# Reordering the four products of a k-tile in an FFN up-projection: wide, narrow, wide, narrow against wide, wide, narrow, narrow

## The chip, the cores and the metric

The kernel runs on one core of one Trainium2 chip, as one program launched once. The metric is the device time of one execution in microseconds. A core has five engines that run their own instruction streams side by side: TensorE (matrix products; in the profile PE, and PEld for the loading of its weights), VectorE (DVE), ScalarE (ACT), GpSimd (POOL), and SyncE (SP), which here issues the transfers from device memory. They wait for one another through semaphores.

## The reference

One layer of a hybrid decoder on 256 tokens of width 2048, in float32. Cut to its steps:

```
h  = rms_norm(x, attn_norm);  z = h @ w_in              # 2048 -> 4384
mix = [causal pooling of z, RWKV-7 time mixing of z]
x  = x + mix @ w_out                                    # 2048 -> 2048
h2 = rms_norm(x, mlp_norm)
x  = x + square(relu(h2 @ w_ffn_up)) @ w_ffn_down       # 2048 -> 8192 -> 2048
gate = sigmoid(rms_norm(x, ple_norm) @ w_ple_gate)
x  = x + gate * (p @ w_ple_proj)
out = rms_norm(x, final_norm)
```

The change touches only `h2 @ w_ffn_up`.

## The kernel before

**Precision.** Every large product is made of three. A float32 operand is split into a high half (rounded to the fast format that TensorE takes, `F32R` in the code) and a low half (the rest), and high x high, high x low and low x high are summed in PSUM, TensorE's accumulator memory, which is divided into banks of 512 float32 columns.

**Staging of weights.** `load_raw` has SyncE bring a panel of 128 x 1024 weights (512 KB) into one of three buffers. `split_w` makes the two halves: ScalarE copies the panel into `wh` in two instructions (line 149), VectorE subtracts to get `wl` in one (line 150). `wh` and `wl` have three buffers each, and the splitting runs at a raised priority, so it goes ahead as far as free buffers allow.

**FFN-up.** `gemm_wide` computes it, transposed: the weights are the stationary operand (128 x 128 at a time) and the normalised activations, already transposed by `transposed("h2")`, are the moving one. A call handles 512 of the 8192 columns, in two halves of 256. For a half, `kq` runs over four panels. A panel holds four k-tiles (a k-tile is 128 of the 2048 rows that are summed over), of 256 columns each. For a k-tile there are two column tiles `ct` of 128 columns, each with two products:

- a wide one (line 997): weights `wh`, moving operand `hl = acts(k)`, the high and low halves of the activations side by side, 256 + 256 columns in two stretches of memory. It writes a whole bank, `bank[:, ct, :]`: high x high in the first 256 columns, high x low in the other 256.
- a narrow one (line 1001): weights `wl`, moving operand the high half alone, 256 columns. It adds to the first 256 columns of the same bank.

The two column tiles have a bank each, and such a pair of banks (`wide_bank`) exists twice, so that one half can be emptied while the next is computed. Each product has a weight load of its own ahead of it; the profile shows these as LDWEIGHTS on PEld.

When a half is done, `consume` (the function `square` in `ffn_half`, lines 1193 and on) lets ScalarE copy the second columns out of the bank, VectorE add the first and apply the squared ReLU, and splits the result for the down-projection.

**Order of the work.** `ffn_half` runs twice. Each time eight calls of `gemm_wide` come first (256 k-tiles, 1024 products), then two calls of `down_sweep`, the down-projection, whose products are all 512 wide (lines 1111 to 1113). These two stretches of `gemm_wide` are called the first and the second FFN half here. Nothing but the loops sets the order around the change. The framework schedules the instructions of each engine by priority and readiness: at the very start of the first FFN half some of the transposes that make `h2` (line 1018) stand between products of lines 997 and 1001.

Other stages used for comparison: `prod_toks` (lines 171 to 173), 512-wide products in the output projection and the gate; `prod_cols` (lines 162 to 164), 256-wide products in the input projection and the pooling; `kept_product` (lines 1266 to 1268), the last gate products, first a run of 512-wide ones, then 256-wide ones.

Of the kernel before, what the change touches and what calls it, by code (L numbers as in the profile page):

```python
# [16 lines left out]
T = 256  # L17
# [23 lines left out]
def trunk(  # L41
# [96 lines left out]
    def load_raw(src, n, name):  # L138
        raw = wp.tile([128, 1024], F32, tag="raw", name=f"raw_{name}")
        nc.sync.dma_start(raw[:, 0:n], src)  # L140
        return raw

    def split_w(raw, name):

        wh = wp.tile([128, 1024], F32R, tag="wh", name=f"wh_{name}")
        wl = wp.tile([128, 1024], F32R, tag="wl", name=f"wl_{name}")
        with tc.high_priority(20000):
            for a in range(2):
                nc.scalar.activation(wh[:, a * 512 : (a + 1) * 512], raw[:, a * 512 : (a + 1) * 512], AF.Copy)  # L149
            nc.vector.tensor_tensor(wl, raw, wh.bitcast(F32), op=ALU.subtract)  # L150
        return [(t_h, t_l) for t_h, t_l in zip((wh[:, 0:512], wh[:, 512:1024]), (wl[:, 0:512], wl[:, 512:1024]))]
# [185 lines left out]
    for kg, (tg, n) in enumerate((("tE", 1), ("tF", 2), ("zk", 3), ("zr", 3), ("zv", 3), ("BK", 2), ("BKt", 2))):  # L337
# [13 lines left out]
        if kg == 4:  # L351
            for tt in range(2):
                for i, q in enumerate((2, 3)):
                    nc.tensor.matmul(
                        sbank[:, tt : tt + 1], sums[q][:, 0, tt * 128 : (tt + 1) * 128], ones[:, 0:1],
                        start=i == 0 and tt == 0, stop=i == 1, skip_group_check=True,
# [623 lines left out]
    def wide_bank(name):  # L980
        return psw.tile([128, 2, 512], F32, tag="wide", name=name)

    def gemm_wide(src, acts, name, consume):

        for half in range(2):
            bank = wide_bank(f"{name}_w{half}")
            for kq in range(4):
                raw = load_raw(src[half, kq].rearrange("p a n -> p (a n)"), 1024, f"{name}{half}_{kq}")  # L990
                for a, (wh, wl) in enumerate(split_w(raw, f"{name}{half}_{kq}")):
                    for b in range(2):
                        k = kq * 4 + 2 * a + b
                        hl = acts(k)
                        for ct in range(2):
                            c = slice(b * 256 + ct * 128, b * 256 + ct * 128 + 128)
                            nc.tensor.matmul(  # L997
                                bank[:, ct, :].rearrange("p (s t) -> p s t", s=2), wh[:, c], hl,
                                start=k == 0, stop=False, skip_group_check=True,
                            )  # L1000
                            nc.tensor.matmul(  # L1001
                                bank[:, ct, 0:T], wl[:, c], hl[:, 0, :], start=False, stop=k == 15, skip_group_check=True
                            )
            consume(half, bank)

# [177 lines left out]
    def ffn_half(hf):  # L1183
        sboxes = {}
        ys = []
        for i in range(8):
            f = hf * 8 + i
            y = fp.tile([128, 2048], F32R, tag="y", bufs=8, name=f"y{f}")

            def square(bi, bank):  # L1190
                r = fp.tile([128, 512], F32, tag="r", bufs=2, name=f"r{f}_{bi}")
                r2 = r.rearrange("p (c t) -> p c t", c=2)
                nc.scalar.activation(r2, bank[:, :, T : 2 * T], AF.Copy)
                nc.vector.tensor_tensor(r2, bank[:, :, 0:T], r2, op=ALU.add)
                nc.vector.scalar_tensor_tensor(r, r, 0.0, r, op0=ALU.max, op1=ALU.mult)
                split_sb(y[:, bi * 512 : bi * 512 + 512], y[:, 1024 + bi * 512 : 1024 + bi * 512 + 512], r)
                if 2 * i + bi in SEVEN:
                    activation_sums(sboxes, 2 * i + bi, r)

            gemm_wide(w_up[f], h2, f"u{f}", square)  # L1200
            ys.append(y)
            if f == 1:
                inv_ms()
# [162 lines left out]
```

## Time and profile before

| what | value |
|---|---|
| time, median of 3 runs | 1199.78 us (1199.17 to 1201.17) |
| the profiled execution: its own time | 1201.35 us |
| the profiled execution: its span | 1199.6 us |
| granted TensorE clock | 0.997 of full speed |
| first product of the first FFN half, first down-projection product behind it | 388.7 us, 567.1 us |
| first product of the second FFN half, first down-projection product behind it | 734.7 us, 915.6 us |

How to read the profile. A row of the groups gives the line, the engine, the operation, what it writes and reads, the shapes and the count; after the bar the busy time in microseconds, the mean duration in nanoseconds, and the idle time of the engine just before these instructions with what ended it. A row of the timeline gives the start in microseconds from the span's start, the duration in microseconds, the engine, the line and the operands. On TensorE the recorded spans of neighbouring products overlap and their ends are modelled, so the pace is read from the distance between starts. The chain that ended last is followed back from the last instruction, and shares are of the span.

### The profile page before, as it was taken

To read this page: it belongs to the slowest core of one execution; us is meant where nothing else is said; L and a number is where in the kernel's file an instruction comes from. 1 tells how busy PE (TensorE), PEld (TensorE's weight loads), DVE (VectorE), ACT (ScalarE), POOL (GpSimd) and SP (SyncE) were. 2 spreads that over 40 slices of the span, in tenths; PEclk is the share of its full clock that TensorE was granted. 3 is DMA by queue.
4 is the path that set the end of the run, shared out by engine and by line. 5 is a ranking of instruction groups with operands and counts; after the bars stand their busy time and mean duration, and the time that the engine had idled before them with its cause. 6 is when DMAs were issued, how large, how long until landed. Compare 5 with 4: busy or idle time off the path is not lost.

```text
span 1199.6 us, 18428 instructions
## 1 busy us (share of the span) xinstructions
PE 1179.5 (98%) x7060; PEld 1010.6 (84%) x7060; DVE 868.5 (72%) x1149; ACT 689.8 (58%) x1276; POOL 18.1 (2%) x69
## 2 busy tenths in 40 slices
PE   8999999999999999999999999999999999999997
PEld 6999988987887888888888788888888888777886
DVE  7687987965656666666878888666667879787552
ACT  6857566566545565555655564454555555668544
POOL 4000010000000000000000000000000000000000
PEclk9999999999999999999999999999999999999999
DMA  6463542354445555555665656655555556766531
GB/s 246 154 201 109 175 144 104 113 198 141 140 163 179 184 185 190 192 191 189 201 201 200 193 195 211 191 181 188 189 184 189 207 194 197 287 231 211 195 120 70
DMA packets 60328, 216.88 MB, mean 181 GB/s; under 512 B 6736, under 2 KB 7120, under 8 KB 59856
## 3 DMA queue, kind: packets, MB, share of 16 engines
q1 hardware_dynamic: 59952, 215.19, 53.4%
q8 instruction: 55, 0.90, 0.3%
q10 hardware_dynamic: 288, 0.52, 0.1%
q14 instruction: 33, 0.27, 0.1%
HBM read 213.59 MB, written 2.10 MB: 180 GB/s over the span
## 4 chain that ended last, share of the span: by engine, by line
PE 81%; DVE 8%; DMA 4%; ACT 4%; issue 2%; SPq 0%; ACTq 0%; DVEq 0%
PE u_w L997 20%; PE u_w L1001 10%; PE d_b L1112 5%; PE d_b L1113 5%; PE d_b L1111 5%; DMA raw_d<-in_w_ffn_down_dram 3%; PE gt_b L171 2%; PE gt_b L173 2%; PE gt_b L172 2%; PE wag_b L331 1%; PE zp_b L171 1%; PE o_b L171 1%; PE o_b L172 1%; PE o_b L173 1%; PE d_w L1112 1%
## 5 line engine op out<-in xcount | busy, mean ns | idle before, releaser
L997 PE MATMUL u_w<-h,wh_u 128*128 128x512 f32 x1024 | 358.8, 395 | 0.0
L1001 PE MATMUL u_w<-h,wl_u 128*128 128x256 f32 x1024 | 287.3, 281 | 0.0
L149 ACT ACTIVATE wh_u<-raw_u 128x512 fp32r<-128x512 f32 x256 | 147.6, 624 | 166.2 <-PE u_w L997 93.1
L150 DVE TENSOR_TENSOR wl_u<-raw_u,wh_u 128x1024 fp32r<-128x1024 f32 x128 | 156.7, 1225 | 115.1 <-ACT wh_u L149 115.1
L997 PEld LDWEIGHTS u_w<-h,wh_u 128*128 128x128 f32 x1024 | 192.0, 187 | 44.8
L1001 PEld LDWEIGHTS u_w<-h,wl_u 128*128 128x128 f32 x1024 | 193.6, 189 | 0.0
L150 DVE TENSOR_TENSOR wl_gt<-raw_gt,wh_gt 128x1024 fp32r<-128x1024 f32 x24 | 29.4, 1225 | 23.9 <-ACT wh_gt L149 23.9
L149 ACT ACTIVATE wh_gt<-raw_gt 128x512 fp32r<-128x512 f32 x48 | 27.8, 631 | 23.0 <-PE gt_b L173 18.8
L1151 DVE TENSOR_TENSOR td<-raw_d 128x512 f32<-128x512 f32 x22 | 15.2, 693 | 31.0 <-DMA raw_d<-in_w_ffn_down_dram 31.0
L162 PE MATMUL zv_b<-hTh,wh_zv 128*128 128x256 f32 x128 | 37.6, 294 | 0.0
L171 PE MATMUL gt_b<-wh_gt,h 128*128 128x512 f32 x96 | 37.5, 390 | 0.0
L162 PE MATMUL zr_b<-hTh,wh_zr 128*128 128x256 f32 x128 | 37.4, 292 | 0.0
L173 PE MATMUL gt_b<-wh_gt,h 128*128 128x512 f32 x96 | 37.4, 389 | 0.0
L172 PE MATMUL gt_b<-wl_gt,h 128*128 128x512 f32 x96 | 37.4, 389 | 0.0
L164 PE MATMUL zr_b<-hTh,wl_zr 128*128 128x256 f32 x128 | 37.0, 289 | 0.1
L163 PE MATMUL zr_b<-hTl,wh_zr 128*128 128x256 f32 x128 | 37.0, 289 | 0.0
L162 PE MATMUL zk_b<-hTh,wh_zk 128*128 128x256 f32 x128 | 36.9, 288 | 0.0
L163 PE MATMUL zk_b<-hTl,wh_zk 128*128 128x256 f32 x128 | 36.3, 284 | 0.5 <-DVE hTl L155 0.5
L164 PE MATMUL zk_b<-hTh,wl_zk 128*128 128x256 f32 x128 | 36.3, 284 | 0.1
L163 PE MATMUL zv_b<-hTl,wh_zv 128*128 128x256 f32 x128 | 36.2, 283 | 0.0
L164 PE MATMUL zv_b<-hTh,wl_zv 128*128 128x256 f32 x128 | 36.2, 283 | 0.0
L154 ACT ACTIVATE wad<-raw_d 128x512 fp32r<-128x512 f32 x22 | 13.9, 632 | 33.7 <-DMA raw_d<-in_w_ffn_down_dram 29.1
(807 smaller groups left out, 3077.6 us busy)
## 6 DMA issues: line engine op xcount, KB each, us to landing
raw_u<-in_w_ffn_up_dram SPq DMA_DIRECT2D x128, 512.0 KB, 3.6
raw_d<-in_w_ffn_down_dram SPq DMA_DIRECT2D x128, 512.0 KB, 4.0
raw_gt<-in_w_ple_gate_dram SPq DMA_DIRECT2D x24, 512.0 KB, 3.5
raw_zk<-in_w_in_dram SPq DMA_DIRECT2D x16, 512.0 KB, 3.3
raw_zr<-in_w_in_dram SPq DMA_DIRECT2D x16, 512.0 KB, 3.4
raw_zv<-in_w_in_dram SPq DMA_DIRECT2D x16, 512.0 KB, 3.2
raw_zp<-in_w_in_dram SPq DMA_DIRECT2D x16, 512.0 KB, 3.3
raw_o<-in_w_out_dram SPq DMA_DIRECT2D x16, 512.0 KB, 3.5
```

The source lines that it names most:

```text
L149: nc.scalar.activation(wh[:, a * 512 : (a + 1) * 512], raw[:, a * 512 : (a + 1) * 512], AF.Copy)
L150: nc.vector.tensor_tensor(wl, raw, wh.bitcast(F32), op=ALU.subtract)
L162: nc.tensor.matmul(o, w_h, ah, start=first and ct % 2 == 0, stop=False, skip_group_check=True)
L163: nc.tensor.matmul(o, w_h, al, start=False, stop=False, skip_group_check=True)
L164: nc.tensor.matmul(o, w_l, ah, start=False, stop=last, skip_group_check=True)
L171: nc.tensor.matmul(o, a_h, wh[:, 0:n], start=first, stop=False)
L172: nc.tensor.matmul(o, a_h, wl[:, 0:n], start=False, stop=False)
L173: nc.tensor.matmul(o, a_l, wh[:, 0:n], start=False, stop=last)
L997: nc.tensor.matmul(bank[:, ct, :].rearrange("p (s t) -> p s t", s=2), wh[:, c], hl, start=k == 0, stop=False, skip_group_check=True,)
L1001: nc.tensor.matmul(bank[:, ct, 0:T], wl[:, c], hl[:, 0, :], start=False, stop=k == 15, skip_group_check=True)
L1111: nc.tensor.matmul(banks[n], ah, wh, start=first, stop=False)
L1112: nc.tensor.matmul(banks[n], ah, wl, start=False, stop=False)
```

## The change

For each k-tile the loop over the two column tiles is split in two: first both wide products, then both narrow ones. Before, the four products of a k-tile go wide (ct 0), narrow (ct 0), wide (ct 1), narrow (ct 1); after, wide (ct 0), wide (ct 1), narrow (ct 0), narrow (ct 1). Into each bank the wide product still goes ahead of the narrow one. Operands, widths, flags and counts are the same.

```diff
                     for b in range(2):
                         k = kq * 4 + 2 * a + b
                         hl = acts(k)
+                        cs = [slice(b * 256 + ct * 128, b * 256 + ct * 128 + 128) for ct in range(2)]
                         for ct in range(2):
-                            c = slice(b * 256 + ct * 128, b * 256 + ct * 128 + 128)
                             nc.tensor.matmul(
-                                bank[:, ct, :].rearrange("p (s t) -> p s t", s=2), wh[:, c], hl,
+                                bank[:, ct, :].rearrange("p (s t) -> p s t", s=2), wh[:, cs[ct]], hl,
                                 start=k == 0, stop=False, skip_group_check=True,
                             )
+                        for ct in range(2):
                             nc.tensor.matmul(
-                                bank[:, ct, 0:T], wl[:, c], hl[:, 0, :], start=False, stop=k == 15, skip_group_check=True
+                                bank[:, ct, 0:T], wl[:, cs[ct]], hl[:, 0, :], start=False, stop=k == 15, skip_group_check=True
                             )
             consume(half, bank)
```

## The prediction

> **What bounds the kernel now.** I began with the page: engine shares, clock, chain, costliest groups.
>
> ```profile
> PE 1179.5 (98%) x7060; PEld 1010.6 (84%) x7060; DVE 868.5 (72%) x1149; ACT 689.8 (58%) x1276; POOL 18.1 (2%) x69
> PEclk9999999999999999999999999999999999999999
> PE 81%; DVE 8%; DMA 4%; ACT 4%; issue 2%; SPq 0%; ACTq 0%; DVEq 0%
> PE u_w L997 20%; PE u_w L1001 10%; PE d_b L1112 5%; PE d_b L1113 5%; PE d_b L1111 5%; DMA raw_d<-in_w_ffn_down_dram 3%; PE gt_b L171 2%; PE gt_b L173 2%; PE gt_b L172 2%; PE wag_b L331 1%; PE zp_b L171 1%; PE o_b L171 1%; PE o_b L172 1%; PE o_b L173 1%; PE d_w L1112 1%
> L997 PE MATMUL u_w<-h,wh_u 128*128 128x512 f32 x1024 | 358.8, 395 | 0.0
> L1001 PE MATMUL u_w<-h,wl_u 128*128 128x256 f32 x1024 | 287.3, 281 | 0.0
> L149 ACT ACTIVATE wh_u<-raw_u 128x512 fp32r<-128x512 f32 x256 | 147.6, 624 | 166.2 <-PE u_w L997 93.1
> L150 DVE TENSOR_TENSOR wl_u<-raw_u,wh_u 128x1024 fp32r<-128x1024 f32 x128 | 156.7, 1225 | 115.1 <-ACT wh_u L149 115.1
> ```
>
> TensorE is busy 98% of the span at full clock, and lines 997 and 1001, the two that the change reorders, hold 30% of the chain that ended last. Neither line ever waits (the last column, 0.0). The engines that feed them do wait: ScalarE sits idle 166.2 us before its 256 weight splits, 93.1 us of it for line 997 to give a buffer back. So in FFN-up only the pace of TensorE's own stream counts, and any nanosecond gained or lost there is a nanosecond of the kernel.
>
> Busy time cannot give that pace, because the recorded spans overlap: 358.8 + 287.3 us is far more than the stage lasts. The pace is the distance between starts. I looked at it in the timeline, three pairs in the first FFN half (near 500 us) and three in the second (near 800 us), and then at the groups by shape over most of either half.
>
> ```profile
> 499.88 0.39 PE L997 MATMUL u_w<-h,wh_u 128*128 128x512 f32 x1
> ...
> 500.92 0.39 PE L997 MATMUL u_w<-h,wh_u 128*128 128x512 f32 x1
> ```
>
> ```profile
> 800.04 0.40 PE L997 MATMUL u_w<-h,wh_u 128*128 128x512 f32 x1
> 800.28 0.28 PE L1001 MATMUL u_w<-h,wl_u 128*128 128x256 f32 x1
> 800.40 0.40 PE L997 MATMUL u_w<-h,wh_u 128*128 128x512 f32 x1
> 800.64 0.28 PE L1001 MATMUL u_w<-h,wl_u 128*128 128x256 f32 x1
> 800.75 0.40 PE L997 MATMUL u_w<-h,wh_u 128*128 128x512 f32 x1
> 800.99 0.28 PE L1001 MATMUL u_w<-h,wl_u 128*128 128x256 f32 x1
> 801.10 0.40 PE L997 MATMUL u_w<-h,wh_u 128*128 128x512 f32 x1
> ```
>
> ```profile
> L997 PE MATMUL u_w<-h,wh_u 128*128 128x512 f32 x491 | 170.3, 391 | 0.0
> L1001 PE MATMUL u_w<-h,wl_u 128*128 128x256 f32 x492 | 137.8, 280 | 0.0
> ```
>
> ```profile
> L997 PE MATMUL u_w<-h,wh_u 128*128 128x512 f32 x505 | 178.5, 399 | 0.0
> L1001 PE MATMUL u_w<-h,wl_u 128*128 128x256 f32 x504 | 141.6, 281 | 0.0
> ```
>
> The first fence is 1.04 us for three pairs: 346.7 ns a pair, 693.3 ns a k-tile (two pairs). The second is 1.06 us: 353.3 ns a pair, 706.7 ns a k-tile; there the distances walk round a cycle of three pairs (0.24, 0.12, 0.24, 0.11, 0.24, 0.11 us). The two group tables (395 to 565 us, then 736 to 914 us) say that this holds all along: the wide product's mean is 391 ns in the one and 399 ns in the other, by the same instructions. So the same code runs at two paces, a settled one and an unsettled one. That is the reading on which everything below rests.
>
> **The change part by part.** The number of products, their widths, weight loads, bytes and DMAs stay. Per k-tile the order wide, narrow, wide, narrow becomes wide, wide, narrow, narrow, on 512 k-tiles (256 in each half). The average pace before is (693.3 + 706.7) / 2 = 700.0 ns, so with c the new distance per k-tile the change is worth 512 x (c - 700.0 ns): every 2 ns of c is 1.0 us.
>
> Neither wide after wide nor narrow after narrow stands in FFN-up before. The nearest rows are elsewhere: long runs of one width, here the last gate products (1174 to 1178 us wide, 1180 to 1186 us narrow), and the places where a run of one width follows the other.
>
> ```profile
> L1267 PE MATMUL gt3a<-gk,h 128*128 128x512 f32 x7 | 2.7, 389 | 0.0
> ```
>
> ```profile
> L1267 PE MATMUL gt3b<-gk,h 128*128 128x256 f32 x14 | 4.0, 283 | 0.0
> ```
>
> ```profile
> 327.95 0.28 PE L164 MATMUL pm<-d,pws 128*128 128x256 f32 x1
> 328.07 0.40 PE L171 MATMUL o2a_b<-wh_o2a,mp 128*128 128x512 f32 x1
> 328.30 0.40 PE L172 MATMUL o2a_b<-wl_o2a,mp 128*128 128x512 f32 x1
> 328.54 0.39 PE L173 MATMUL o2a_b<-wh_o2a,mp 128*128 128x512 f32 x1
> ```
>
> ```profile
> 1178.05 0.39 PE L1268 MATMUL gt3a<-gk,h 128*128 128x512 f32 x1
> ...
> 1178.73 0.39 PE L1268 MATMUL gt3a<-gk,h 128*128 128x512 f32 x1
> 1178.96 0.28 PE L1266 MATMUL gt3b<-gk,h 128*128 128x256 f32 x1
> 1179.07 0.28 PE L1267 MATMUL gt3b<-gk,h 128*128 128x256 f32 x1
> 1179.19 0.28 PE L1268 MATMUL gt3b<-gk,h 128*128 128x256 f32 x1
> ...
> 1179.55 0.28 PE L1268 MATMUL gt3b<-gk,h 128*128 128x256 f32 x1
> ```
>
> A settled wide run goes at (1178.73 - 1178.05) / 3 = 227 ns, a settled narrow run at (1179.55 - 1179.19) / 3 = 120 ns. Two of each make 693.3 ns: exactly the settled pace of the alternating order. So the settled price of a product does not depend on its neighbour, and the order alone cannot go below 693.3 ns. This is the low end: c = 693.3, worth 512 x (-6.7) = -3.4 us. It also says that the wide product's moving operand, which line 997 reads in two separate stretches of 256, costs nothing there.
>
> Out of a settled run the first products of the other width are different. After narrow ones the first two wide take 328.54 - 328.07 = 0.47 us, some 16 ns more than settled; after wide ones the first two narrow take 1179.19 - 1178.96 = 0.23 us, some 10 ns less. The new order is a change of width every two products, so its k-tile by these rows is 0.47 + 0.23 = 0.70 us. The starts are rounded to 10 ns, and the recorded durations give the next digit, since a duration is the distance to the next start plus about 162.5 ns (389 and 227, 283 and 120):
>
> ```profile
> L172 PE MATMUL o2a_b<-wl_o2a,mp 128*128 128x512 f32 x1 | 0.4, 398 | 0.0
> L171 PE MATMUL o2a_b<-wh_o2a,mp 128*128 128x512 f32 x1 | 0.4, 396 | 0.0
> ```
>
> ```profile
> L1267 PE MATMUL gt3b<-gk,h 128*128 128x256 f32 x14 | 4.0, 283 | 0.0
> L1266 PE MATMUL gt3b<-gk,h 128*128 128x256 f32 x1 | 0.3, 278 | 0.0
> ```
>
> 396 + 398 + 278 + 283 - 4 x 162.5 = 705 ns by the durations, 700 ns by the starts; I take 702 ns. The high end for c: the longest distances of the unsettled cycle (800.04 to 800.28 and 800.28 to 800.40 us) for every product, 2 x 240 + 2 x 120 = 720 ns, worth +10.2 us; 706.7 ns, the unsettled pace as it stands, is the nearer of the high values. I choose 702 because only these rows have the new order's own neighbours.
>
> Sum: first half 256 x (702 - 693.3) = +2.2 us, second half 256 x (702 - 706.7) = -1.2 us, together +1.0 us.
>
> The weight loads. One load goes with each product, before and after. Its row starts with the product ahead of it and not sooner:
>
> ```profile
> 500.11 0.28 PE L1001 MATMUL u_w<-h,wl_u 128*128 128x256 f32 x1
> 500.11 0.19 PEld L997 LDWEIGHTS u_w<-h,wh_u 128*128 128x128 f32 x1
> ```
>
> So each wide product covers one load and each narrow one covers one, in either order; the new order changes which load lies under which product, not how many lie under a narrow one. Cost nothing; if the loads did not fit under the narrow ones, the narrow runs at 120 ns would show it, and they have a load each.
>
> The Trainium skill (TensorE: Matmul & The Clock Gate, Part 2, step 1 LDWEIGHTS) has TensorE pull weight loads ahead of running products through a window of 64. By that rule loads would gather under the two wide products and narrow ones would go at their bare pace; the trace does not agree, since the load above starts at 500.11 us with the product just ahead of it.
>
> Waits at the edges of a panel. The low weight half is first needed after two wide products instead of one, 0.23 us later; the high half is released one narrow product (0.12 us) sooner. Neither product has a wait to shorten (0.0 above), so this is worth nothing. The cover is ScalarE's idle time of 166.2 us ahead of its splits; if it were gone, each of the 128 panels would come up to 0.12 us sooner by the earlier release, 15 us in all, a gain that the 0.0 excludes. The PSUM bank's evacuation may start 0.12 us sooner; with two banks and 16 k-tiles (11 us) a half, nobody waits for it. No DMA is moved. Cost nothing.
>
> The profiled execution took 1201.35 us for a span of 1199.6 us; by the sum it becomes 1202.4 us. It lies 1.6 us above the median of the runs, 1199.78 us, so the median becomes 1200.8 us.
>
> **The rivals.** What a measurement of this kernel can tell from no change is 0.2%, 2.4 us, which by 512 x (c - 700) is c below 695.3 or above 704.7 ns.
>
> *The new order settles* in both halves, c = 693.3: 1199.8 - 3.4 = 1196.4 us. For it: every long run of one width settles, and runs of two are nearer to that than alternation. Against it: alternation settles only in the first half, and a fresh change of width every two products is what unsettles the rows above.
>
> *The unsettled cycle takes both halves*, the case on the other side: two wide in a row at the unsettled mean, 399 - 162.5 = 236.5 ns, and narrow ones at the 117 to 120 ns that they have everywhere, c about 706.7 to 713. The place is the first half, which loses its settled pace: 256 x 13.3 = +3.4 us, 1203.2 us, and 1206.4 us at 713. It decides from c = 704.7. For it: the second half does this now, for all its 1024 products. Against it: the transition rows at 700 to 705.
>
> *Loads run ahead* under two wide products, so that narrow ones go at the 113 ns that one has after a wide one (278 - 162.5 = 115.5, 0.11 us by starts): c = 2 x 227 + 2 x 113 = 680, -10.2 us, 1189.6 us. Against it: the load row, and the narrow run returning to 120 ns at once. This is the time that the Trainium skill's window (the page and step above) would allow.
>
> *The order isn't carried out*: the framework schedules TensorE's instructions and may move them. Then 1199.8 us. Against it: the pairs stand in the trace as written.
>
> **How the numbers follow.** Forecast (c about 702, 698 to 707): 0.41, most of it within 0.2%, 0.06 of it slower. Settled in both halves: 0.25. Unsettled in both halves or worse: 0.28. Loads run ahead: 0.03. Not carried out: 0.03. Faster by over 0.2%: 0.25 + 0.03 = 0.28. Within: 0.35 + 0.03 = 0.38. Slower: 0.06 + 0.28 = 0.34. The likeliest is 1200.8 us, with 1198.8 to 1203.4 us as its own range (c 698 to 707). The range of 8 in 10 goes from just under the settled case, 1196.0 us, to 1205.5 us (c about 711), which leaves out the run-ahead case and the dear end of the unsettled one.
>
> **What would show it.** In the groups, lines 997 and the narrow line keep 1024 products each and no idle time. In the timeline a k-tile of four starts spans about 0.70 us, with wide distances of 0.23 to 0.24 us and narrow ones of 0.11 and 0.12 us. Right: both halves at the same pace, the first slower than before and the second faster. Wrong: a wide mean of 389 to 391 ns in both halves (settled), or 399 ns and more in both; a load that starts two products ahead; or idle time that appears before the narrow line.

## The result, and the profile after

| | before | after |
|---|---|---|
| median of 22 runs each | 1200.68 us | 1198.38 us |
| ratio after / before, 95% interval | | 0.9978 (0.9968 to 0.9988) |
| the profiled execution, its span | 1201.35 us, 1199.6 us | 1198.69 us, 1197.0 us |
| first FFN half, first start to first down-projection start | 388.74 to 567.13: 178.4 us | 388.75 to 567.95: 179.2 us |
| second FFN half, likewise | 734.69 to 915.58: 180.9 us | 735.07 to 913.40: 178.3 us |

The kernel became 0.22% faster (0.12 to 0.32%, so 1.4 to 3.8 us of 1200). The forecast was 1200.8 us, 1.0 us more than before and too little to be told from no change.

The page after, the lines that answer to those shown of before (engine shares, chain by line, groups):

```profile
PE 1177.8 (98%) x7060; PEld 1008.1 (84%) x7060; DVE 868.4 (73%) x1149; ACT 689.2 (58%) x1276; POOL 18.6 (2%) x69
PE u_w L997 20%; PE u_w L1002 10%; PE d_b L1113 5%; PE d_b L1112 4%; PE d_b L1114 4%; DMA raw_d<-in_w_ffn_down_dram 4%; PE gt_b L171 2%; PE gt_b L173 2%; PE gt_b L172 2%; PE wag_b L331 1%; PE zp_b L171 1%; PE o_b L171 1%; PE o_b L172 1%; PE o_b L173 1%; PE zp_b L173 1%
L997 PE MATMUL u_w<-h,wh_u 128*128 128x512 f32 x1024 | 321.6, 395 | 0.0
L149 ACT ACTIVATE wh_u<-raw_u 128x512 fp32r<-128x512 f32 x256 | 147.6, 624 | 164.4 <-PE u_w L997 93.9
L1002 PE MATMUL u_w<-h,wl_u 128*128 128x256 f32 x1024 | 201.5, 278 | 0.0
```

The narrow product is now line 1002. The busy times fell from 358.8 to 321.6 us and from 287.3 to 201.5 us, and this says nothing: busy time is the union of spans within a group, and products of one line now overlap each other. The other rows are those of before: 1024 products each, no idle time, ScalarE waiting 164.4 us (166.2).

The pace is in the starts. The timeline of after near 800 us; it merges the two products of a kind into one row:

```profile
799.85 0.63 PE L997 MATMUL u_w<-h,wh_u 128*128 128x512 f32 x2
800.32 0.39 PE L1002 MATMUL u_w<-h,wl_u 128*128 128x256 f32 x2
800.54 0.63 PE L997 MATMUL u_w<-h,wh_u 128*128 128x512 f32 x2
801.01 0.40 PE L1002 MATMUL u_w<-h,wl_u 128*128 128x256 f32 x2
801.24 0.63 PE L997 MATMUL u_w<-h,wh_u 128*128 128x512 f32 x2
```

Two wide ones take 0.47 us, two narrow ones 0.22 and 0.23 us: two k-tiles in 1.39 us. The groups by shape over most of either half (395 to 565 us, then 736 to 912 us) hold the same means:

```profile
L997 PE MATMUL u_w<-h,wh_u 128*128 128x512 f32 x489 | 153.6, 395 | 0.0
L1002 PE MATMUL u_w<-h,wl_u 128*128 128x256 f32 x489 | 96.1, 278 | 0.0
```

```profile
L997 PE MATMUL u_w<-h,wh_u 128*128 128x512 f32 x506 | 158.9, 395 | 0.0
L1002 PE MATMUL u_w<-h,wl_u 128*128 128x256 f32 x506 | 99.4, 278 | 0.0
```

395 and 278 ns in both halves: one pace, where before had 391 and 280 in the first and 399 and 281 in the second. For the size, the whole of the second half, from its first wide product to the first down-projection product behind it:

```profile
735.07 0.61 PE L997 MATMUL u_w<-h,wh_u 128*128 128x512 f32 x2
...
913.40 0.40 PE L1112 MATMUL d_b<-wh_d_0a,y 128*128 128x512 f32 x1
```

178.33 us for 256 k-tiles: 696.6 ns each, with c = 696.7 ns in the steady part of either half. The first half lost 0.8 us (178.4 to 179.2), the second gained 2.6 us (180.9 to 178.3): 1.7 us from FFN-up together, or 0.15% of the kernel, inside the measured interval. The two profiled executions differ by 2.66 us; the other 0.9 us is before, between and after the halves, and by the repeats below such a difference is no more than two executions of one program show.

### The profile page after: what moved, and what is told of

It reads as the page before. It is cut to its first block, busy times and chain, and to the rows that moved or that the text cites. A ratio compares the mean times of both kernels' runs of the same rounds, so it can differ in the third digit from the quotient of the medians.

```text
span 1197.0 us, 18432 instructions
## 1 busy us (share of the span) xinstructions
PE 1177.8 (98%) x7060; PEld 1008.1 (84%) x7060; DVE 868.4 (73%) x1149; ACT 689.2 (58%) x1276; POOL 18.6 (2%) x69
## 4 chain that ended last, share of the span: by engine, by line
PE 78%; DVE 9%; DMA 6%; ACT 5%; issue 2%; SPq 0%; ACTq 0%; DVEq 0%
PE u_w L997 20%; PE u_w L1002 10%; PE d_b L1113 5%; PE d_b L1112 4%; PE d_b L1114 4%; DMA raw_d<-in_w_ffn_down_dram 4%; PE gt_b L171 2%; PE gt_b L173 2%; PE gt_b L172 2%; PE wag_b L331 1%; PE zp_b L171 1%; PE o_b L171 1%; PE o_b L172 1%; PE o_b L173 1%; PE zp_b L173 1%
## 5 line engine op out<-in xcount | busy, mean ns | idle before, releaser
L997 PE MATMUL u_w<-h,wh_u 128*128 128x512 f32 x1024 | 321.6, 395 | 0.0
L149 ACT ACTIVATE wh_u<-raw_u 128x512 fp32r<-128x512 f32 x256 | 147.6, 624 | 164.4 <-PE u_w L997 93.9
L1002 PE MATMUL u_w<-h,wl_u 128*128 128x256 f32 x1024 | 201.5, 278 | 0.0
L997 PEld LDWEIGHTS u_w<-h,wh_u 128*128 128x128 f32 x1024 | 155.9, 189 | 0.1
```

The source lines that it names most:

```text
L997: nc.tensor.matmul(bank[:, ct, :].rearrange("p (s t) -> p s t", s=2), wh[:, cs[ct]], hl, start=k == 0, stop=False, skip_group_check=True,)
L1002: nc.tensor.matmul(bank[:, ct, 0:T], wl[:, cs[ct]], hl[:, 0, :], start=False, stop=k == 15, skip_group_check=True)
```

## The experiments

A theory was set against four rivals. The theory: only the sequence of widths counts, through the pace at which TensorE takes the products. The rivals: the bank that a narrow product adds to, the two-stretch operand, the supply of weights, and the entry into a half. In the table, FFN-up is the sum of both halves in the profiled execution, from the timeline as above (the added transposes included); the ratio is against runs of before on the same chip; the paces are the distances of starts over 192 k-tiles of a half, behind its first 32.

| run | k-tile, first half | k-tile, second half | FFN-up, against 359.3 us | ratio of times |
|---|---|---|---|---|
| after | 696.7 ns | 696.7 ns | -1.7 us | 0.9978 (0.9968 to 0.9988) |
| runs of four | 701.7 | 701.7 | +0.7 us | 1.0002 (0.9986 to 1.0019) |
| runs of eight | 698.3 | 698.3 | -0.8 us | 0.9985 (0.9969 to 1.0001) |
| other bank | 706.2 | 706.2 | +3.0 us | 1.0019 (1.0007 to 1.0031) |
| one stretch | 693.3 | 706.7 | 0.0 us | 1.0006 (0.9986 to 1.0026) |
| 1 transpose | 693.3 | 706.7 | +0.2 us | 0.9995 (0.9981 to 1.0010) |
| 2 transposes | 693.3 | 693.3 | -3.2 us | 0.9975 (0.9951 to 1.0000) |
| 3 transposes | 693.3 | 706.7 | +0.3 us | 1.0005 (0.9987 to 1.0024) |
| 6 transposes | 693.3 | 693.3 | -2.7 us | 0.9988 (0.9973 to 1.0003) |

**Runs of four and of eight.** For two k-tiles, or for a panel of four, first all wide products and then all narrow ones (the edit for runs of four, abridged):

```diff
-                    for b in range(2):
-                        (wide ct 0, narrow ct 0, wide ct 1, narrow ct 1)
+                    four = [(k, ct, c) for b in range(2) for ct in range(2)]
+                    for k, ct, c in four:
+                        wide(k, ct, wh[:, c])
+                    for k, ct, c in four:
+                        narrow(k, ct, wl[:, c])
```

> The same products with runs of four: for two k-tiles of a panel all four wide products, then all four narrow ones. Theory (the pace is set by how a stream of two widths settles, and each change of width unsettles it): half as many changes of width as after the change, so a k-tile takes 693.3 to 696.7 ns in both FFN halves, and the kernel is 1.7 to 3.4 us faster than before. Rival bank (a narrow product is dear right behind the wide one of its own bank): the bank changes with each product as it does after the change, so 696.7 ns in both halves, as after. Rival supply (what counts is when the weight halves are released and first needed): the low half is needed 0.45 us later still, so faster than after by up to as much again as the change gave, about 4.5 us against before. Rival entry (what precedes a half decides, by chance): either of 693.3 and about 707 ns, not the same in both halves.

> Runs of eight: all eight wide products of a panel, then all eight narrow ones. Theory: a quarter of the changes of width, so at most the pace of runs of four, close to 693.3 ns a k-tile in both halves, and 3 to 3.4 us faster than before. Rival bank: 696.7 ns, as after. Rival supply: faster again than runs of four, since the low weight half is first needed eight products into the panel. Rival entry: 693.3 or about 707 ns by chance.

The timeline of runs of four, then of runs of eight (in these two kernels line 991 is the wide product and line 997 the narrow one):

```profile
800.13 0.63 PE L997 MATMUL u_w<-h,wl_u 128*128 128x256 f32 x4
800.60 1.09 PE L991 MATMUL u_w<-h,wh_u 128*128 128x512 f32 x4
801.53 0.64 PE L997 MATMUL u_w<-h,wl_u 128*128 128x256 f32 x4
```

```profile
800.37 2.00 PE L991 MATMUL u_w<-h,wh_u 128*128 128x512 f32 x8
802.21 1.11 PE L997 MATMUL u_w<-h,wl_u 128*128 128x256 f32 x8
803.16 1.09 PE L991 MATMUL u_w<-h,wh_u 128*128 128x512 f32 x4
```

This part of the theory fell: fewer changes of width did not bring the pace towards 693.3 ns step by step. Runs of four are at 701.7 ns, slower than runs of two, and runs of eight at 698.3. A change of width has no fixed price; it sets off a transient that runs on over several products. Eight wide ones take 802.21 - 800.37 = 1.84 us, 0.03 us more than eight settled ones (8 x 226.7 ns = 1.81), and eight narrow ones take 0.95 us, 0.01 us less (8 x 120 = 0.96). Four wide ones already take 0.93 us, 0.02 us more than settled (0.91). So most of the price falls in the first four wide products. By the paces, a full round of runs costs, over settled, 4 x (698.3 - 693.3) = 20.0 ns with runs of eight, 2 x (701.7 - 693.3) = 16.8 ns with runs of four, but only 3.4 ns with runs of two, and 6.7 ns (half of 706.7 - 693.3) in the unsettled alternation. Runs of two change width again before the transient has come out. That alone would put them at the 702 ns of the prediction's rows; why they are cheaper still, no run shows.

The rival supply is out as well. With runs of four the low weight half is needed later than after the change, and FFN-up is 2.5 us longer than after (+0.7 against -1.7).

**Other bank.** Widths alternate, but each narrow product is the one of the bank that the wide product ahead of it did not write (the order in short):

```diff
-   wide(k, 0);  narrow(k, 0);    wide(k, 1);  narrow(k, 1)
+   wide(k, 0);  narrow(k-1, 1);  wide(k, 1);  narrow(k, 0)      # and narrow(15, 1) at the end of the half
```

> Widths alternate as before, but each narrow product adds to the bank that the wide product just ahead of it did not write (wide ct 0, narrow ct 1 of the k-tile before, wide ct 1, narrow ct 0). Theory: only the sequence of widths counts, so the paces are those of before, 693.3 or 706.7 ns a k-tile in each half, and the time is that of before within 0.3%. Rival bank: the cost of the unsettled pace goes, so 696.7 ns or less in both halves and 1.7 us or more faster than before. Rival entry: the same numbers as the theory, but settled and unsettled halves may change places.

It is 0.19% slower than before (0.07 to 0.31%), and almost all of it goes unsettled, but not because of the bank: a stretch of the first half (about 394 to 400.8 us, its end shown here; line 991 is the wide product, 997 the narrow one) settles with the banks crossed.

```profile
399.84 0.39 PE L991 MATMUL u_w<-h,wh_u 128*128 128x512 f32 x1
400.07 0.28 PE L997 MATMUL u_w<-h,wl_u 128*128 128x256 f32 x1
400.19 0.39 PE L991 MATMUL u_w<-h,wh_u 128*128 128x512 f32 x1
400.42 0.28 PE L997 MATMUL u_w<-h,wl_u 128*128 128x256 f32 x1
400.53 0.39 PE L991 MATMUL u_w<-h,wh_u 128*128 128x512 f32 x1
400.76 0.40 PE L997 MATMUL u_w<-h,wl_u 128*128 128x256 f32 x2
```

Two pairs in 0.69 us is the settled pace. It ends where a half of a call ends (the last row): there two narrow products stand in a row, and behind them the stream stays unsettled (398 and 281 ns by the groups, 410 to 565 us). The 706.2 ns of the table are the unsettled cycle of 706.7 with this disturbance every 16 k-tiles in it. So the same two paces, 693.3 and 706.7 ns, appear whichever bank the narrow product adds to; the bank is out as a cause, and something as small as one extra narrow product can tip the stream from one into the other.

**One stretch.** The order of before, with the activations laid out so that the wide product's 512 moving columns are contiguous:

```diff
-        hl = fp.tile([128, 2, NK, T], F32R, tag="h2", name=name)
-        h, l = hl[:, 0], hl[:, 1]
+        hl = fp.tile([128, NK, 2, T], F32R, tag="h2", name=name)
+        h, l = hl[:, :, 0, :], hl[:, :, 1, :]
...
-        return part, lambda k: hl[:, :, k, :]
+        return part, lambda k: hl[:, k, :, :]
```

> The order of before, with the activations laid out so that the high and low halves of a k-tile are next to each other: the wide product's moving operand is one stretch of 512 columns instead of two of 256. Theory: the paces are those of before, 693.3 in the first half and 706.7 ns in the second. Rival two stretches (the two-stretch operand is what unsettles the stream): 693.3 ns in both halves, 3.4 us faster than before.

The paces are those of before to 0.1 ns, and so is the length of FFN-up. The operand's two stretches are out. (The first half settles here in another form, 394 and 277 ns by the groups against 391 and 280, at the same sum. The runs with one and two transposes below do so too, with the operand in its two stretches, so the layout isn't what picks the form.)

**The entry.** Transposes of 128 x 128, whose results nobody reads, ahead of the calls of the up-projection, a different number ahead of each; once with the order of before and once with that of after:

```diff
+            if f % 8:
+                filler = mm_bank(f"filler{f}")
+                for j in range(f % 8 if f < 8 else 4 + f % 8):
+                    nc.tensor.transpose(filler[:, j % 4 * 128 : j % 4 * 128 + 128], xr[0][:, 0:128], ident)
             gemm_wide(w_up[f], h2, f"u{f}", square)
```

> The order of before, with 128-wide transposes into an unused bank put ahead of the calls of the up-projection: call f (0 to 15) gets f of them up to 7, none at 8, then 4 + f - 8, so 5 to 11. They change nothing of the result; they cost about 0.11 us each, and only the pace inside each call is read. Theory (alternating widths repeat one of two patterns, and the entry decides which): within one run some calls go at 693.3 ns a k-tile and others at 706.7, in either half, and the pace changes only at a call with transposes ahead of it. Rival place (the second half is slower through something else that goes on there): calls 0 to 7 at 693.3, 8 to 15 at 706.7, whatever stands ahead of them.

> The order after the change with the same transposes ahead of the calls. Theory: the order wide, wide, narrow, narrow has one pattern only, so every call goes at 696.7 ns a k-tile from a few products in. Rival entry (the change only drew another entry): calls at different paces, 693.3 or 706.7 among them.

Order of before, the groups within four calls of the second half: call 9 (5 transposes ahead; 762 to 783 us), call 10 (6; 785 to 806 us), call 14 (10; 878 to 899 us), call 15 (11; 901 to 922 us):

```profile
L997 PE MATMUL u_w<-h,wh_u 128*128 128x512 f32 x60 | 21.2, 399 | 0.0
```

```profile
L997 PE MATMUL u_w<-h,wh_u 128*128 128x512 f32 x62 | 21.5, 391 | 0.0
```

```profile
L997 PE MATMUL u_w<-h,wh_u 128*128 128x512 f32 x61 | 21.6, 399 | 0.0
```

```profile
L997 PE MATMUL u_w<-h,wh_u 128*128 128x512 f32 x62 | 21.6, 392 | 0.0
```

Within one execution the calls go at either pace, and within a half it changes only at calls with transposes ahead. By the steady part of each call, calls 4 and 5 of the first half went at 706.7 ns and the others at 693.3; in the second half calls 8, 9 and 14 at 706.7 and the others at 693.3. Five transposes led to the unsettled pace both times, six and seven to the settled one both times. The number alone doesn't decide, though: four led to the unsettled pace in call 4, while in the first half of every run of before's order the stream is settled behind four transposes of `h2`. The rival place is out: the second half is no slower as such. With the order of after, all 16 calls went at 696.6 to 696.9 ns whatever stood ahead of them. So the change did not only draw another entry; its order has one pace, where alternation has two. (The transposes of calls 1 and 2 and one of call 3 were scheduled ahead of the stage's first product, so the 16 calls are 14 entries: call 0 and calls 3 to 15.)

**The same programs once more.**

> The kernel before once more. If the pattern follows from the program alone: 693.3 ns a k-tile in the first half and 706.7 in the second again. If it is drawn anew in each execution: any of the two in either half, and the spread of the run times (1196.7 to 1204.9 us) would come in part from that, in steps of 3.4 us.

> The kernel after the change once more: 696.7 ns a k-tile in both halves again by the theory, whatever the time of this execution.

Before, again, in its second half (736 to 910 us), has the unsettled 399 and 281 ns; its steady paces are 693.3 and 706.7 ns as the first time, and after's are 696.7 twice:

```profile
L997 PE MATMUL u_w<-h,wh_u 128*128 128x512 f32 x494 | 174.6, 399 | 0.0
L1001 PE MATMUL u_w<-h,wl_u 128*128 128x256 f32 x493 | 138.5, 281 | 0.0
```

In the second half, behind the unbroken stream of the down-projection, the pace follows from the program. At the start of the first half the pattern does not. Seven pairs stand there between transposes. Here are three of them in before, and three in the run with one transpose below (where lines 1000 and 1004 are the products), whose instructions are the same up to the second half:

```profile
390.54 0.40 PE L997 MATMUL u_w<-h,wh_u 128*128 128x512 f32 x1
...
391.60 0.40 PE L997 MATMUL u_w<-h,wh_u 128*128 128x512 f32 x1
```

```profile
389.38 0.39 PE L1000 MATMUL u_w<-h,wh_u 128*128 128x512 f32 x1
...
390.42 0.39 PE L1000 MATMUL u_w<-h,wh_u 128*128 128x512 f32 x1
```

That is 1.06 us, unsettled, against 1.04 us, settled. Of six executions with these instructions four are unsettled there (before twice, three and six transposes) and two settled (one and two). Between the run with two and that with six, the starts ahead of these pairs, counted from the stage's first product, differ by 3 ns at most; so a few ns at the entry, or something that the trace doesn't show, is enough to choose. Behind the four transposes that follow, all six go at 693.3 ns.

This execution of before had a span of 1197.1 us against 1199.6 us the first time, with FFN-up at 359.3 us in both, so what spreads the run times lies elsewhere, and 0.9 us between two executions needs no cause in the change.

**Settling the second half of before.** One, two, three or six transposes ahead of its first product (shown with two):

```diff
             bank = wide_bank(f"{name}_w{half}")
+            if name == "u8" and half == 0:
+                for _ in range(2):
+                    nc.tensor.transpose(bank[:, 0, 0:128], xr[0][:, 0:128], ident)
```

> The order of before, with one 128-wide transpose ahead of the first product of the second FFN half, into the bank that this product then overwrites. The first half is untouched (693.3 ns a k-tile). Theory: the entry alone decides the pattern of the second half; the number of transposes that settles it can't be worked out from the trace, so either 706.7 ns in the whole half and 0.1 us slower than before, or 693.3 ns in the whole half and 256 x 13.4 ns = 3.4 us less, minus 0.1 us for the transpose, 3.3 us faster. Rival (the gain of the change has nothing to do with the pace of the products): the time stays that of before even where the half settles.

> As with one transpose, with two: 706.7 ns and 0.2 us slower than before, or 693.3 ns and about 3.2 us faster. With the rival, the time of before in both cases.

> As with one transpose, with three: 706.7 ns and 0.3 us slower than before, or 693.3 ns and about 3.0 us faster. With the rival, the time of before in both cases.

> As with one transpose, with six, the number behind which two calls of the entry run went at the settled pace: 693.3 ns in the whole second half and 3.4 - 0.7 = 2.7 us faster than before, if the number alone counts; 706.7 ns and 0.7 us slower, if it counts as well that 512-wide products stand ahead of it here. With the rival, 0.7 us slower in any case.

The entry with two transposes (line 991; line 1000 is the wide product and 1004 the narrow one), then the groups of that half (736 to 910 us) with two and with one:

```profile
733.38 0.39 PE L1116 MATMUL d_b<-wh_d_15b,y 128*128 128x512 f32 x1
733.61 0.38 PE L991 MATMUL u_w<-ident,x 128*128 128x128 f32 x2
733.74 0.48 PE L1000 MATMUL u_w<-h,wh_u 128*128 128x512 f32 x1
734.06 0.28 PE L1004 MATMUL u_w<-h,wl_u 128*128 128x256 f32 x1
734.18 0.39 PE L1000 MATMUL u_w<-h,wh_u 128*128 128x512 f32 x1
```

```profile
L1000 PE MATMUL u_w<-h,wh_u 128*128 128x512 f32 x503 | 174.4, 391 | 0.0
```

```profile
L1000 PE MATMUL u_w<-h,wh_u 128*128 128x512 f32 x493 | 174.2, 399 | 0.0
```

Two and six settle the whole half, one and three don't: the number's effect isn't monotone, as in the entry run. With two, FFN-up is 3.2 us shorter than before, as expected, and the time is 0.25% less (0.49% less to no change): the estimate agrees with the 3.2 us (0.27%), though its interval just reaches no change. The three others move by their own FFN-up sums within their intervals, which include no change. Taken together, the 21 executions of the two programs that settle (two and six) have a median of 1198.04 us, against 1200.28 us of the 24 that don't (one and three): 2.2 us less (0.3 to 4.0 by resampling). The grouping was made after the fact, but it speaks against the rival, by which the gain has nothing to do with the pace. So the order of before with two transposes in the right place has a shorter FFN-up than the change (356.1 against 357.5 us); that it beats the change in time wasn't compared directly, and their intervals overlap.

## Why the prediction was wrong

**What bounds the kernel** held: a TensorE stream without idle time, at two paces before, 30% of the chain. Every run's FFN-up follows from its pace, and 512 x (c - 700.0 ns) with the measured c gives 512 x (-3.3) = -1.7 us, what the two halves show.

**The floor** held: no order tried goes below 693.3 ns in its steady part, and the two-stretch operand costs nothing. The reason given for the floor, that a product's settled price doesn't depend on its neighbour, did not hold: by the starts in nanoseconds, settled alternation is 230 for the wide and 117 for the narrow product, against 227 and 120 in runs of one width. Only the sum is the same.

**The step that failed is the choice of c**, "Out of a settled run the first products of the other width are different ... I take 702 ns". The shape of the sum held: both halves got one pace, the first lost and the second gained, as the forecast said. The term c was mis-sized by 5.3 ns a k-tile, 2.7 us in all: the first half's term was +0.8 us instead of +2.2, the second's -2.6 instead of -1.2. The rows themselves were read well: by their starts in nanoseconds the first two wide products take 233 + 236 = 469 ns and the first two narrow ones 114 + 119 = 233, together 702 (that the 705 of the durations and the 700 of the rounded starts lie on either side of it is luck). The fault was to put the steady k-tile together from products that follow a settled run, since in the steady stream no run starts from a settled one. There the pairs take, in turn, 469.3 (wide), 228.3 (narrow), 463.3 (wide) and 232.4 ns (narrow): every second pair of a width costs what the rows say, the others some 5 ns less. That makes 1393.3 ns for two k-tiles, 696.7 each. Why every second pair is cheaper stays open. Behind settled runs, as in runs of eight, the transient comes out in full, 20.0 ns a round; cut after two products of each width it would be 8.7 (702 - 693.3), and runs of two pay 3.4. My own range for c, 698 to 707, did not reach 696.7.

**No effect from waits, banks and weight supply** held: idle time stayed 0.0, the split engines kept their slack, and the runs that changed bank and need of the low half showed no effect of either. The idle column alone would not show a short wait, since the recorded spans overlap by some 160 ns; the starts do: behind the first 32 k-tiles of a half no distance exceeds 241 ns in before or 236 ns in after, the longest of the regular cycles.

**The rivals.** "The new order settles" was nearest in time (1196.4 us) and in sign, but it isn't what happened: c is 696.7, not 693.3, at all 14 entries tried. What the prediction set against it, that alternation settles only in the first half, was rightly read as two states; what I did not consider is that the entry alone picks the state, so that before's second half could be settled without any reordering. "Loads run ahead" is out: the narrow pairs at 0.22 to 0.23 us and wide ones at 0.47 us leave 696.7 ns, not 680. That time was what I had drawn from the Trainium skill's page TensorE: Matmul & The Clock Gate (Part 2, step 1), which has weight loads pulled ahead of running products. The prediction went too far in saying that the trace does not agree: each load does start while the product ahead of it runs. But in after all but three load rows behind a product of FFN-up start 2 to 5 ns behind the start of the product just ahead (those three 77 to 84 ns), so none shows a lead of more than one product.

**The sign.** With at least 0.12% of gain, +1.0 us had the wrong sign, and it follows from c alone: the sign turns at c = 700.0 ns, between my 702 and the measured 696.7. FFN-up accounts for 0.15% of the 0.22%; what is left lies within the interval.

## What to carry to other kernels

Where TensorE runs without idle time, read its pace from the distance of starts, stage by stage, before asking what hides what: the same instructions can repeat at two paces (here 1.9% apart), and the order of widths and even a single product at the entry choose between them. A transient seen behind a long run of one kind isn't the price in a stream that changes kind every few products, and not a bound on it either: by the same rows (233 + 114 ns a pair) alternation would be at 694 ns a k-tile, and it was at 693.3 or 706.7. That has to be measured. An order with one pace whatever stands ahead of it can be worth having even if its pace isn't the lowest.

## What the runs showed of the hardware that was not expected

- A stream of alternating 512-wide and 256-wide products, each with its own weight load, repeated one of three patterns: starts 230 and 117 ns apart; 233, 118, 231 and 112 ns (both 693.3 ns for two pairs); or the cycle of three pairs at 706.7 ns. It stayed in one for up to 1024 products.
- In the second half, behind an unbroken stream of 512-wide products, the pattern of before was the same in both its executions, and the transposes of 128 columns put ahead changed it: 2 or 6 led to 693.3 ns, 0, 1 or 3 to 706.7. The number alone doesn't decide (four led to either pace), and at the start of the first half executions of the same instructions differed.
- The pace does not improve steadily with the length of equal runs: 696.7 ns with two, 701.7 with four, 698.3 with eight.
- What in TensorE carries the pattern from product to product stays open. The bank, the operand's layout and the supply of weights were excluded; the weight loads were not separated from the products, since every product here has its own.
